# Hybrid decoder trunk: pacing of the last tail, copied scores, and the order of the last four blocks

## The chip, the cores and the metric

The kernel runs on one core of a Trainium2 chip. Time is the device time of one execution in microseconds. The kernel before takes 3587.44 us, the median of three runs (3582.51, 3587.91 and 3587.44). Smaller is better.

## The reference

One pre-norm residual layer over 1024 tokens of width 1024, then a final RMS norm:

```python
h = rms_norm(x, norm_mix[l])
x = x + hybrid_mixer(h, ...)          # stick-breaking attention, sparse attention, HGRN2, gated merge, w_out
h = rms_norm(x, norm_ffn[l])
x = x + peer_ffn(h, peer_w_q[l], peer_sub_keys[l], peer_u[l], peer_v[l])
...
return rms_norm(x, norm_final)
```

The second half is what the change touches. It is a product-key expert layer: each token picks, for each of 8 heads, 16 of 16384 experts, by the 16 best of 128 keys on each of two sides and then the 16 best of the 256 sums.

```python
s = jnp.einsum("nhad,akd->nhak", qh, sub_keys).astype(f32)
top_s, top_i = lax.top_k(s, K)
...
best_s, pos = lax.top_k(cand, K)
eidx = jnp.take_along_axis(cand_idx, pos, axis=-1)
gate = jax.nn.softmax(best_s, axis=-1)
hpre = jnp.einsum("nd,nhkd->nhk", xc, u_tab[eidx]).astype(f32)
act = (gate * jax.nn.gelu(hpre, approximate=False)).astype(x.dtype)
return jnp.einsum("nhk,nhkd->nd", act, v_tab[eidx])
```

## The kernel before

The tokens are four parts of 256 (`PARTS`), eight tiles of 128. The mixer runs first, part by part, as stages whose pieces (projections, norms, scores, routing) are emitted by due times of TensorE and VectorE work; a tail of a part is its merge, output projection, norm, scores and routing. The tail of the last part has nothing of the mixer to lie beside: its 68 steps (8 merges, 22 of projection and norm, 16 of scores, 22 of routing) are put into the list `ending` and handed out during the expert layer.

`score_pieces` makes, for each head, the scores `zs` of two tiles against 128 keys on two sides in PSUM (L973), and VectorE finds the 16 best of each: maximum of eight (L978), their replacement into an SBUF tile `sv` (L980), their indices (L982), and the same again on `sv` (L984, L986). A head has four such sets, so each line runs 128 times over the four parts.

The expert layer is done in two ways. The 512 tokens of parts 1 and 2 (`DENSE`) go over all 16384 experts in 128 blocks of 128: `gemm1` (matmuls at L258, 24 of 128x512 a block, fp16 high and low halves) gives 128 hidden values of 512 tokens, ScalarE takes the Gelu `ge` (L1390), VectorE multiplies it by the gates `gt` (L1424, two instructions), ScalarE and VectorE split it into two fp16 halves `ac` (L213, L214) and the block of `peer_v` likewise into `vs`, and `gemm2` (L1431) adds to the output. `gemm1` runs `LEAD` = 3 blocks ahead. Token tiles 0 to 2 keep their sums in six PSUM banks `accs`; the fourth, for which there is no bank, collects four blocks (`group`), is multiplied in a bank shared with `gemm1`, copied out by ScalarE as `p7` (L1440) and added to `acc7` by VectorE (L1441). At the end the sums are scaled and added to the residual (`yd`, L1460), normed and scaled by `norm_final` (L1462), and stored.

The other 512 tokens (tiles 0, 1, 6, 7 of 128) are done by `gather_tile`, beside the blocks: for each of 128 choices GpSimd gathers 128 rows of `peer_u` by an indirect DMA (L1145, 512 KB), VectorE takes the dot product with the token (L1147); then the same with rows of `peer_v` (L1155), each scaled and added to `gacc` (L1157). Then the sum is normed and multiplied by `norm_final` (L1162) and stored. Rows, the sums `gacc`, the copies of the tokens and `gf` take buffers of the tag `rows`, of which there are five; for tiles 6 and 7 `late_rows` adds seven more places that the mixer has left (names with `rr_` are halves of one of them), in a ring of eleven in which four turns fall to `rows`.

The program is written in this order and a scheduler with a model of the engines arranges the instructions of each engine within what buffers and dependencies allow; VectorE's steps on rows are held back by `paced` to spread them over the blocks. In the loop over blocks, `TP` = 3 steps of `ending` are emitted behind each block. `account` adds a model cost of each VectorE instruction emitted to `load_["DVE"]`. `W2` tiles (the tag `at`, eight buffers) hold `ge`, `sv`, `p7` and the routing's tables.

## Time and profile before

| | |
|---|---|
| median of three runs | 3587.44 us |
| profiled execution | 3598.97 us, span 3597.2 us |
| TensorE busy | 3273.4 us, 91% |
| VectorE busy | 3002.8 us, 83% |
| ScalarE busy | 1588.9 us, 44% |
| GpSimd busy | 1342.3 us, 37% |
| `ac127` to the end | 45.5 us |

The profile lists one execution. Busy time is time in which an engine worked on an instruction; a TensorE that is busy need not run at its peak. The blocks of the expert layer fill the span from about 2150 us on. A wait is put down to the instruction that ended last among those waited for.

### The profile page before, as it was taken

What the parts mean: (1) busy time and instruction counts of PE and PEld (TensorE: products, weight loads), DVE (VectorE), ACT (ScalarE), POOL (GpSimd) and SP (SyncE); (2) the same over time, 40 slices, a digit from 0 to 9 for tenths busy, and PEclk for the clock granted to TensorE, in tenths of its full rate; (3) what the DMA queues carried; (4) which work ended last, traced back from release to release, by engine and by line L of the source; (5) the groups of instructions that cost most, each with busy time, mean ns of one, the idle gap of its engine ahead of it and who ended that gap; (6) DMA issues with size and microseconds to landing.
All of it is one profiled execution on the core that took longest, in us unless ns stands there. A gap on an engine that the chain in (4) does not pass through costs nothing.

```text
span 3597.2 us, 57076 instructions
## 1 busy us (share of the span) xinstructions
PE 3273.4 (91%) x20660; PEld 2191.4 (61%) x20660; DVE 3002.8 (83%) x6662; ACT 1588.9 (44%) x3157; POOL 1342.3 (37%) x1166
## 2 busy tenths in 40 slices
PE   7999989989997889999878879879999999999997
PEld 6887777778875667787666645434444444444443
DVE  5565678888799878788997777999897998898898
ACT  5776455653443554645356333224233333333333
POOL 0000002343323323223332233346674765666664
PEclk9999999999996889999677789989999999999998
DMA  8964856989977577887665799789998999999997
GB/s 300 329 237 143 303 185 224 329 300 328 351 259 230 198 248 244 306 320 261 218 201 184 265 348 316 240 270 374 358 369 316 383 378 343 379 358 364 352 343 263
DMA packets 358760, 1053.88 MB, mean 293 GB/s; under 512 B 35174, under 2 KB 107562, under 8 KB 354380
## 3 DMA queue, kind: packets, MB, share of 16 engines
q0 software_dynamic: 147456, 536.94, 41.7%
q1 hardware_dynamic: 211020, 513.29, 40.2%
q8 instruction: 162, 2.65, 0.3%
q14 instruction: 122, 1.00, 0.1%
HBM read 942.09 MB, written 108.00 MB: 292 GB/s over the span
## 4 chain that ended last, share of the span: by engine, by line
PE 44%; DVE 24%; DMA 11%; issue 10%; ACT 7%; POOL 4%; SPq 0%; POOLq 0%; DVEq 0%; ACTq 0%
PE g L258 11%; PE acc L1431 8%; DVE u L1147 4%; PE pj_mg L258 3%; DVE gacc L1157 3%; PE g L1431 3%; DMA d_G<-stage 3%; PE pj_r_hg L258 3%; DMA v<-in_peer_v_dram,gidx 2%; PE pb L258 2%; DMA u<-in_peer_u_dram,gidx 2%; PE pj_wo L258 2%; POOL v L1155 2%; DMA gt<-d_G 1%; POOL u L1145 1%
## 5 line engine op out<-in xcount | busy, mean ns | idle before, releaser
L1155 POOL DMA_INDIRECT v<-in_peer_v_dram,gidx x421 | 541.5, 1286 | 723.1 <-DVE gacc L1157 435.6
L1145 POOL DMA_INDIRECT u<-in_peer_u_dram,gidx x417 | 523.7, 1256 | 683.2 <-DVE u L1147 440.2
L258 PE MATMUL g<-h,us 128*128 128x512 f16 x3072 | 692.0, 382 | 26.3 <-DVE ts L982 10.3
L1157 DVE SCALAR_TENSOR_TENSOR gacc<-v,act,gacc 128x1024 f32<-128x1024 f32 x421 | 538.5, 1279 | 35.1 <-DMA v<-in_peer_v_dram,gidx 31.6
L1431 PE MATMUL acc<-vs,ac 128*128 128x512 f16 x2304 | 540.3, 383 | 23.1 <-DVE vs L214 9.7
L1431 PEld LDWEIGHTS <-ac 128*128 128x128 f16 x3072 | 303.2, 99 | 419.2 <-issue 58.7
L258 PEld LDWEIGHTS <-us 128*128 128x128 f16 x3072 | 302.1, 98 | 395.3 <-issue 24.8
L1147 DVE SCALAR_TENSOR_TENSOR u<-u,gh 128x1024 f32<-128x1024 f32 x417 | 501.6, 1218 | 33.1 <-DMA u<-in_peer_u_dram,gidx 30.0
L1390 ACT ACTIVATE ge<-g 128x512 f32<-128x512 f32 x128 | 76.2, 595 | 570.6 <-PE g L258 528.2
L258 PE MATMUL pj_mg<-hT,w_mg 128*128 128x256 f16 x2304 | 276.3, 276 | 8.8 <-ACT mg L883 7.0
L258 PEld LDWEIGHTS <-w_mg 128*128 128x128 f16 x2304 | 228.7, 100 | 40.1 <-issue 12.6
L1431 PE MATMUL g<-vs,ac 128*128 128x512 f16 x768 | 187.4, 386 | 24.6 <-ACT ge L1390 23.0
L1221 ACT ACTIVATE stage<-gb 128x512 f32<-128x512 f32 x128 | 130.3, 1070 | 125.3 <-DMA d_G<-stage 59.9
L214 DVE SCALAR_TENSOR_TENSOR vs<-vraw,vs 128x1024 f16<-128x1024 f32 x128 | 155.5, 1218 | 35.5 <-ACT vs L213 35.3
L213 ACT ACTIVATE vs<-vraw 128x1024 f16<-128x1024 f32 x128 | 133.0, 1046 | 82.4 <-DMA vraw<-in_peer_v_dram 79.6
L258 PE MATMUL pb<-o,w_b 128*128 128x256 f16 x1152 | 147.8, 286 | 21.4 <-DVE sg L921 12.7
L1145 POOL DMA_INDIRECT rr_u<-in_peer_u_dram,gidx x95 | 132.6, 1396 | 85.6 <-DVE rr_u L1147 62.7
L1155 POOL DMA_INDIRECT rr_v<-in_peer_v_dram,gidx x90 | 128.6, 1428 | 95.5 <-DVE gacc L1157 72.4
L214 DVE SCALAR_TENSOR_TENSOR us<-uraw,us 128x1024 f16<-128x1024 f32 x128 | 155.9, 1218 | 9.8 <-ACT us L213 9.4
L1218 PE MATMUL gb<-hot 128*128 128x128 f16 x512 | 125.3, 294 | 42.1 <-ACT stage L1221 22.3
L213 ACT ACTIVATE ac<-ge 128x512 f16<-128x512 f32 x128 | 79.7, 627 | 176.0 <-DVE ge L1424 122.3
L1424 DVE TENSOR_TENSOR ge<-ge,gt 128x256 f32<-128x256 f32 x256 | 98.6, 422 | 68.0 <-ACT ge L1390 46.2
(1143 smaller groups left out, 6439.4 us busy)
## 6 DMA issues: line engine op xcount, KB each, us to landing
uraw<-in_peer_uT_dram SPq DMA_DIRECT2D x128, 512.0 KB
vraw<-in_peer_v_dram SPq DMA_DIRECT2D x128, 512.0 KB
w_mg<-dw SPq DMA_DIRECT2D x72, 512.0 KB
d_G<-stage SPq DMA_DIRECT2D x32, 1024.0 KB
gt<-d_G SPq DMA_DIRECT2D x32, 1024.0 KB
w_r_hg<-dw SPq DMA_DIRECT2D x36, 512.0 KB
w_b<-dw SPq DMA_DIRECT2D x72, 256.0 KB
wr_mg<-in_wblk_dram SPq DMA_DIRECT2D x24, 512.0 KB
```

The lines of the kernel that those rows point to most:

```text
L213: S.activation(hi, src, AF.Copy, scale=scale)
L214: V.scalar_tensor_tensor(lo, in0=src, scalar=scale, in1=hi, op0=ALU.mult, op1=ALU.subtract)
L258: P.matmul(ps, l[:, k, :], r[:, k, :], start=(i == 0), stop=(i == n - 1))
L1145: G.indirect_dma_start(out=ur, out_offset=None, in_=a["peer_u"], in_offset=bass.IndirectOffsetOnAxis(ap=idx[:, c:c + 1], axis=0))
L1147: V.scalar_tensor_tensor(ur, in0=ur, scalar=1.0, in1=h2, op0=ALU.mult, op1=ALU.mult, accum_out=hpre[:, c:c + 1])
L1155: G.indirect_dma_start(out=vr, out_offset=None, in_=a["peer_v"], in_offset=bass.IndirectOffsetOnAxis(ap=idx[:, c:c + 1], axis=0))
L1157: V.scalar_tensor_tensor(acc, in0=vr, scalar=act[:, c:c + 1], in1=acc, op0=ALU.mult, op1=ALU.add)
L1218: P.matmul(ps[:, n, :], hs[:, 0, :, n], hs[:, 2, :, n], start=True, stop=False)
L1221: S.activation(stage[0][:, :, m0:m0 + 4].rearrange("p i n -> p n i"), ps, AF.Copy, scale=SA / SGT)
L1390: S.activation(ge, ps, AF.Gelu, scale=1.0 / (SW * SH2))
L1424: V.tensor_tensor(gv, gv, gt[:, :, i % 8, :], op=ALU.mult)
L1431: P.matmul(ps, ac[:, x, t * 128:(t + 1) * 128], v[:, y, dh * 512:(dh + 1) * 512], start=start and n == 0, stop=stop and n == 2)
```

## The change

There are four parts. First, ScalarE copies the scores `zs` out of PSUM into a new SBUF tile `zc`, and VectorE's searches read that. Second, steps of `ending` are handed out by VectorE's model cost: at most `TP` behind a block, and only while those of this block have cost less than `TV` = 6.0 (an excess is carried into the next block). Third, the last four blocks (124 to 127) have no second products of their own: behind block 126 the products of tiles 3 and 0 with blocks 124 to 126 are made, behind block 127 those of tiles 3 and 0 with block 127 and then all four blocks for tiles 1 and 2; the final sums follow in the order 3, 0, 1, 2. Fourth, tiles 6 and 7 take `gfd`, the row `norm_final` that the dense tiles load in the last block, in place of a load of their own into a `rows` buffer.

```diff
--- before.py
+++ after.py
@@ -25,7 +25,8 @@
 
 PACE0, PACE, PB = 135, 420, 3.0
 
-TP, LEAD = 3, 3
+
+TP, TV, LEAD = 3, 6.0, 3
 
 EVERY = 2
 
@@ -972,6 +973,9 @@
             for tl in range(pt.nt):
                 P.matmul(zs[:, tl, :], st["pq", h][:, tl * 128:(tl + 1) * 128], keys, start=True, stop=True)
 
+            zc = W2(f"zc{pt.i}_{h}", (128, pt.nt, 256))
+            S.activation(zc, zs, AF.Copy)
+            zs = zc
             sv = W2(f"sv{pt.i}_{h}", (128, pt.nt, 256))
             four = [(zs[:, tl, x * 128:x * 128 + 128], sv[:, tl, x * 128:x * 128 + 128], st["ts"][:, tl, h, x, :], st["ti"][:, tl, h, x, :]) for tl in range(pt.nt) for x in range(2)]
             for z, v, t, i in four:
@@ -1158,7 +1162,7 @@
         with tc.high_priority():
             log_exp()
         y = rms_scale(acc, f"fin{ti}", rows(f"sqf{ti}"), "g")
-        gf = load(rows(f"gf{ti}"), a["norm_final"].to_broadcast([128, D]))
+        gf = gfd if ti // 2 == PARTS[-1].i else load(rows(f"gf{ti}"), a["norm_final"].to_broadcast([128, D]))
         V.scalar_tensor_tensor(acc, in0=acc, scalar=y, in1=gf, op0=ALU.mult, op1=ALU.mult)
         nc.sync.dma_start(out[ti * 128:(ti + 1) * 128, :], acc)
 
@@ -1405,7 +1409,8 @@
 
     gts = {}
     ys = []
-    gone = 0
+    spare = 0.0
+    pend = {}
     for k, i in enumerate(order):
         if k + LEAD < NI:
             ges[order[k + LEAD]] = gemm1(order[k + LEAD])
@@ -1430,7 +1435,22 @@
             for n, (x, y) in enumerate(((0, 0), (0, 1), (1, 0))):
                 P.matmul(ps, ac[:, x, t * 128:(t + 1) * 128], v[:, y, dh * 512:(dh + 1) * 512], start=start and n == 0, stop=stop and n == 2)
 
-        for u in range(6):
+        if k >= NI - 4:
+
+            last = k == NI - 1
+            for t in ((3, 0) if k == NI - 2 else (3, 0, 1, 2) if last else ()):
+                for dh in range(2):
+                    if t == 3 and dh not in pend:
+                        pend[dh] = ps_mm.tile([128, TH], F32, tag="mm", name=f"g2_{i}_{dh}")
+                    ps = pend[dh] if t == 3 else accs[t * 2 + dh]
+                    todo_ = group if t in (1, 2) else group[3:] if last else group
+                    for x, y in todo_:
+                        gemm2(ps, t, dh, x, y, t == 3 and x is group[0][0], last and x is ac)
+                    if t == 3 and last:
+                        part = W2(f"p7_{i}_{dh}")
+                        S.activation(part, ps, AF.Copy)
+                        V.tensor_tensor(acc7[:, dh], acc7[:, dh], part, op=ALU.add)
+        for u in range(6 if k < NI - 4 else 0):
             if u in (2, 4) and len(group) == 4:
                 d0 = u // 2 - 1
                 ps = ps_mm.tile([128, TH], F32, tag="mm", name=f"g2_{i}_{u}")
@@ -1449,11 +1469,15 @@
                 ys.append(load(W4("yd3"), d_x2[DENSE[0].ti0 + 3]))
                 gfd = load(late.tile([128, D], F32, tag="v", name="gfd", bufs=6), a["norm_final"].to_broadcast([128, D]))
 
-        while ending and gone < (k + 1) * TP:
-            ending.pop(0).emit(1 << 20)
-            gone += 1
+        account()
+        spare, left = TV + min(spare, 0.0), load_["DVE"]
+        for _ in range(TP):
+            if ending and spare > load_["DVE"] - left:
+                ending.pop(0).emit(1 << 20)
+                account()
+        spare -= load_["DVE"] - left
     log_exp()
-    for t in range(4):
+    for t in (3, 0, 1, 2):
         y = ys[t]
         for dh in range(2):
             yv = y[:, dh * 512:(dh + 1) * 512]
```

Line numbers in the changed kernel are up to 24 higher: the dot products are at L1151, the sums of v rows at L1161, the last scaling at L1166, the gates at L1429, the splits at L214 (ScalarE) and L215 (VectorE).

The first place is VectorE's list beside blocks 17 and 18, where the routing of tile 6 (`rt6`, L1042 to L1064) and the sum of tile 1 (`gacc_1`) go. Before, the multiplication of block 18's Gelu by its gates stands here:

```order
L1058 CAST selh0_rt6_24739<-fb_rt6_24439 128x128
L1047 CAST fa_rt6_24438<-ua_rt6_24440 128x128
L1157 SCALAR_TENSOR_TENSOR gacc_1_33887<-v1_117_34240,act_1_33499,gacc_1_33887 128x1024
L1060 TENSOR_TENSOR oneh0_rt6_24741<-selh0_rt6_24739,iota16r_138 128x2048
L1048 COPY_PREDICATED fb_rt6_24439<-ua_rt6_24440,fa_rt6_24438 128x128
L1157 SCALAR_TENSOR_TENSOR gacc_1_33887<-v1_118_34243,act_1_33499,gacc_1_33887 128x1024
L1062 TENSOR_TENSOR oneh0_rt6_24741<-oneh0_rt6_24741,tir0_rt6_24737 128x2048
L1058 CAST selh1_rt6_24750<-fb_rt6_24439 128x128
L1016 MAX_INDEX ua_rt7_24827<-fa_rt7_24825,cand0_rt7_24828 128x8 x4
L1424 TENSOR_TENSOR ge18_24853<-ge18_24853,gt16_0_25013 128x256
L1424 TENSOR_TENSOR ge18_24853<-ge18_24853,gt16_16_25015 128x256
```

In the changed kernel these rows stand about the same multiplication:

```order
L1161 SCALAR_TENSOR_TENSOR gacc_1_33951<-v1_104_34265,act_1_33563,gacc_1_33951 128x1024
L1047 TENSOR_SCALAR ua_rt6_24596<-ua_rt6_24596 128x128
L1161 SCALAR_TENSOR_TENSOR gacc_1_33951<-v1_105_34268,act_1_33563,gacc_1_33951 128x1024
L1048 TENSOR_SCALAR fa_rt6_24594<-ua_rt6_24596 128x128
L1161 SCALAR_TENSOR_TENSOR gacc_1_33951<-v1_106_34271,act_1_33563,gacc_1_33951 128x1024
L1429 TENSOR_TENSOR ge18_24883<-ge18_24883,gt16_0_25034 128x256
L1049 COPY_PREDICATED fb_rt6_24595<-ua_rt6_24596,fa_rt6_24594 128x128
L1050 TENSOR_SCALAR ua_rt6_24596<-ua_rt6_24596 128x128
L1429 TENSOR_TENSOR ge18_24883<-ge18_24883,gt16_16_25036 128x256
L215 SCALAR_TENSOR_TENSOR us22_25267<-uraw22_25265,us22_25267 128x1024
L1161 SCALAR_TENSOR_TENSOR gacc_1_33951<-v1_107_34274,act_1_33563,gacc_1_33951 128x1024
L1051 CAST fa_rt6_24594<-ua_rt6_24596 128x128
```

and these about that of block 19:

```order
L1027 MAX_INDEX ua_rt7_24983<-fa_rt7_24981,cand0_rt7_24984 128x8 x4
L1161 SCALAR_TENSOR_TENSOR gacc_1_33951<-v1_115_34298,act_1_33563,gacc_1_33951 128x1024
L1062 CAST selh0_rt6_24803<-fb_rt6_24595 128x128
L1051 CAST fa_rt6_24594<-ua_rt6_24596 128x128
L1429 TENSOR_TENSOR ge19_24997<-ge19_24997,gt16_0_25034 128x256
L1429 TENSOR_TENSOR ge19_24997<-ge19_24997,gt16_16_25036 128x256
L1161 SCALAR_TENSOR_TENSOR gacc_1_33951<-v1_116_34301,act_1_33563,gacc_1_33951 128x1024
L1064 TENSOR_TENSOR oneh0_rt6_24805<-selh0_rt6_24803,iota16r_138 128x2048
L1052 COPY_PREDICATED fb_rt6_24595<-ua_rt6_24596,fa_rt6_24594 128x128
L215 SCALAR_TENSOR_TENSOR ac19_25302<-ge19_24997,ac19_25302 128x512
```

The multiplication of `ge18` stood behind the last table step on `fb_rt6` before the one-hot tables; it now stands in the first half of these steps, and `ge19` stands where `ge18` did.

The second place is VectorE's list where tile 6 is scaled by `norm_final` (the row with `gy_fin6`). Before:

```order
L214 SCALAR_TENSOR_TENSOR vs76_29177<-vraw76_29175,vs76_29177 128x1024
L225 TENSOR_SCALAR gms_fin6_35033<-gss_fin6_35030 128x1
L214 SCALAR_TENSOR_TENSOR vs77_29237<-vraw77_29235,vs77_29237 128x1024
L230 TENSOR_TENSOR gu_fin6_35038<-gy_fin6_35035 128x1
L231 TENSOR_TENSOR gu_fin6_35038<-gu_fin6_35038,gms_fin6_35033 128x1
L232 TENSOR_SCALAR gu_fin6_35038<-gu_fin6_35038 128x1
L233 TENSOR_TENSOR gy_fin6_35035<-gy_fin6_35035,gu_fin6_35038 128x1
L1162 SCALAR_TENSOR_TENSOR gacc_6_34665<-gacc_6_34665,gy_fin6_35035,gf6_35043 128x1024
L1424 TENSOR_TENSOR ge78_29051<-ge78_29051,gt72_0_28904 128x256
```

and in the changed kernel:

```order
L215 SCALAR_TENSOR_TENSOR vs126_32551<-vraw126_32549,vs126_32551 128x1024
L215 SCALAR_TENSOR_TENSOR ac126_32556<-ge126_32403,ac126_32556 128x512
L1161 SCALAR_TENSOR_TENSOR gacc_7_35481<-rr_v7_82_35715,act_7_35117,gacc_7_35481 128x1024
L215 SCALAR_TENSOR_TENSOR vs127_32601<-vraw127_32599,vs127_32601 128x1024
L1461 TENSOR_TENSOR acc7_23115<-acc7_23115,p7_123_4_32486 128x512
L1166 SCALAR_TENSOR_TENSOR gacc_6_34729<-gacc_6_34729,gy_fin6_35099,gfd_32679 128x1024
L1161 SCALAR_TENSOR_TENSOR gacc_7_35481<-rr_v7_82_35715,act_7_35117,gacc_7_35481 128x1024
L1429 TENSOR_TENSOR ge127_32495<-ge127_32495,gt120_0_32256 128x256
L1429 TENSOR_TENSOR ge127_32495<-ge127_32495,gt120_16_32258 128x256
L1161 SCALAR_TENSOR_TENSOR gacc_7_35481<-rr_v7_84_35720,act_7_35117,gacc_7_35481 128x1024
```

The scaling stood between blocks 77 and 78 and took a row `gf6`; it now takes `gfd` and stands between the splits of block 126 and the gates of block 127, so that `gacc_6` keeps its buffer until there.

The third place is VectorE's list from the split `ac127` on, the last that TensorE waits for. The names `v7_113` and `rr_v7_84` are rows of the last tile, counted from 0 to 127; a name with `rr_` stands for two neighbouring rows. Before:

```order
L1157 SCALAR_TENSOR_TENSOR gacc_7_35419<-v7_112_35737,act_7_35055,gacc_7_35419 128x1024
L214 SCALAR_TENSOR_TENSOR vs124_32465<-vraw124_32463,vs124_32465 128x1024
L214 SCALAR_TENSOR_TENSOR ac127_32558<-ge127_32431,ac127_32558 128x512
L1157 SCALAR_TENSOR_TENSOR gacc_7_35419<-v7_113_35740,act_7_35055,gacc_7_35419 128x1024
L1157 SCALAR_TENSOR_TENSOR gacc_7_35419<-v7_114_35743,act_7_35055,gacc_7_35419 128x1024
L214 SCALAR_TENSOR_TENSOR vs125_32493<-vraw125_32491,vs125_32493 128x1024
L1157 SCALAR_TENSOR_TENSOR gacc_7_35419<-rr_v7_115_35746,act_7_35055,gacc_7_35419 128x1024 x2
L1157 SCALAR_TENSOR_TENSOR gacc_7_35419<-rr_v7_117_35751,act_7_35055,gacc_7_35419 128x1024 x2
L1157 SCALAR_TENSOR_TENSOR gacc_7_35419<-v7_119_35756,act_7_35055,gacc_7_35419 128x1024
```

and in the changed kernel:

```order
L1161 SCALAR_TENSOR_TENSOR gacc_7_35481<-rr_v7_84_35720,act_7_35117,gacc_7_35481 128x1024
L215 SCALAR_TENSOR_TENSOR ac127_32606<-ge127_32495,ac127_32606 128x512
L1161 SCALAR_TENSOR_TENSOR gacc_7_35481<-rr_v7_84_35720,act_7_35117,gacc_7_35481 128x1024
L1161 SCALAR_TENSOR_TENSOR gacc_7_35481<-v7_86_35725,act_7_35117,gacc_7_35481 128x1024
L1161 SCALAR_TENSOR_TENSOR gacc_7_35481<-v7_87_35728,act_7_35117,gacc_7_35481 128x1024
L1161 SCALAR_TENSOR_TENSOR gacc_7_35481<-v7_88_35731,act_7_35117,gacc_7_35481 128x1024
L1452 TENSOR_TENSOR acc7_23115<-acc7_23115,p7_127_0_32612 128x512
L1161 SCALAR_TENSOR_TENSOR gacc_7_35481<-v7_89_35734,act_7_35117,gacc_7_35481 128x1024
L1484 SCALAR_TENSOR_TENSOR yd0_32547<-acc0_23109,yd0_32547 128x512
L1452 TENSOR_TENSOR acc7_23115<-acc7_23115,p7_127_1_32618 128x512
```

Row 113 was the first behind `ac127`; now it is row 85. The rest of the list to row 127 stands behind it in both, the last 25 rows of the changed kernel without another instruction between them.

## Rows read from the trace of the kernel before

**Rows 1.** The page's first part: busy time of each engine over the whole span, its share, and the number of instructions.

```profile
PE 3273.4 (91%) x20660; PEld 2191.4 (61%) x20660; DVE 3002.8 (83%) x6662; ACT 1588.9 (44%) x3157; POOL 1342.3 (37%) x1166
```

**Rows 2.** The span cut into stretches. Columns: start and end, length, busy time (and number of instructions) of TensorE, of its weight loads, of VectorE, ScalarE and GpSimd, then the granted clock of TensorE, the busy share of the DMA engines and GB/s. The stretches end at the splits `ac` of blocks 19, 31, 119 and 127 on VectorE.

```profile
2280.40:2416.80 136.40, 103.55 (x479) 49.07 (x478) 131.84 (x405) 36.94 (x48) 54.75 (x41) 0.87 0.77 249
2416.80:2541.30 124.50, 120.24 (x551) 54.10 (x550) 122.48 (x250) 48.42 (x65) 81.92 (x60) 0.99 0.97 358
2541.30:3463.70 922.40, 908.37 (x4186) 410.53 (x4185) 828.80 (x1106) 304.83 (x405) 586.16 (x409) 0.99 0.97 359
3463.70:3551.70 88.00, 82.36 (x372) 36.66 (x371) 78.99 (x83) 23.21 (x32) 51.99 (x41) 0.98 0.93 332
3551.70:3597.20 45.50, 22.10 (x88) 9.16 (x87) 37.69 (x60) 14.37 (x27) 7.35 (x8) 0.75 0.51 203
```

**Rows 3.** TensorE's timeline, its last instructions. Columns: start, duration, engine, line, operation, tiles, sizes, count, and in brackets the idle time before it with what ended it.

```profile
3579.62 1.03 PE L1431 MATMUL acc<-vs,ac 128*128 128x512 f16 x4
```

**Rows 4.** VectorE's timeline from block 127's split to the end; columns as in rows 3.

```profile
3549.41 1.28 DVE L1157 SCALAR_TENSOR_TENSOR gacc<-v,act,gacc 128x1024 f32<-128x1024 f32 x1
3550.60 1.22 DVE L214 SCALAR_TENSOR_TENSOR vs<-vraw,vs 128x1024 f16<-128x1024 f32 x1
3551.74 0.68 DVE L214 SCALAR_TENSOR_TENSOR ac<-ge,ac 128x512 f16<-128x512 f32 x1
...
3561.31 6.57 DVE L1157 SCALAR_TENSOR_TENSOR gacc<-v,act,gacc 128x1024 f32<-128x1024 f32 x5
...
3592.09 1.28 DVE L1462 SCALAR_TENSOR_TENSOR yd<-yd,y_find,gfd 128x1024 f32<-128x1024 f32 x1
```

**Rows 5.** TensorE's timeline from 2245 to 2435 us, the groups ahead of which it idled or which ran slowly, and one that did neither (2410.93); columns as in rows 3.

```profile
2251.79 5.35 PE L1431 MATMUL g<-vs,ac 128*128 128x512 f16 x24 [1.64 <-DVE ts L982]
...
2290.47 2.78 PE L258 MATMUL pj_pq<-h_last,w_pq 128*128 128x256 f16 x24 [0.69 <-ACT ge L1390]
...
2317.79 7.44 PE L258 MATMUL g<-h,us 128*128 128x512 f16 x24 [10.27 <-DVE ts L982]
...
2391.15 5.28 PE L1431 MATMUL g<-vs,ac 128*128 128x512 f16 x12 [21.89 <-ACT ge L1390]
2396.23 3.21 PE L1431 MATMUL acc<-vs,ac 128*128 128x512 f16 x12
...
2410.93 5.34 PE L258 MATMUL g<-h,us 128*128 128x512 f16 x24
...
2428.30 6.79 PE L258 MATMUL g<-h,us 128*128 128x512 f16 x24 [4.26 <-ACT ge L1390]
```

**Rows 6.** ScalarE's waits from 2105 us to the end. Columns: what waits, what for, us in total, times, the longest.

```profile
ACT vs L213 <- DMA vraw<-in_peer_v_dram: 79.6, 26, 12.0
...
ACT ge L1390 <- DVE fb_rt L1048: 26.6, 1, 26.6
```

**Rows 7.** VectorE's groups from 3551.7 us to the end. Columns: line, engine, operation, out<-in, sizes, count, busy time, mean ns of one, idle time before them.

```profile
L1460 DVE SCALAR_TENSOR_TENSOR yd<-acc,yd 128x512 f32<-128x512 f32 x8 | 5.3, 685 | 1.1 <-PE acc L1431 1.1
L1462 DVE SCALAR_TENSOR_TENSOR yd<-yd,y_find,gfd 128x1024 f32<-128x1024 f32 x4 | 5.0, 1280 | 0.0
...
L1441 DVE TENSOR_TENSOR acc<-acc,p 128x512 f32<-128x512 f32 x2 | 1.4, 684 | 0.0
L1162 DVE SCALAR_TENSOR_TENSOR gacc<-gacc,gy_fin,gf 128x1024 f32<-128x1024 f32 x1 | 1.3, 1282 | 0.0
```

**Rows 8.** ScalarE's timeline, the steps on the last gathered tile's sum of squares; columns as in rows 3.

```profile
3575.22 1.06 ACT L223 ACTIVATE sqf<-gacc 128x1024 f32<-128x1024 f32 x1 [9.38 <-DVE gacc L1157]
...
3579.19 0.20 ACT L228 ACTIVATE gy_fin<-gy_fin 128x1 f32<-128x1 f32 x1
```

**Rows 9.** The page's fifth part, GpSimd's issues of gathered v rows; columns as in rows 7.

```profile
L1155 POOL DMA_INDIRECT v<-in_peer_v_dram,gidx x421 | 541.5, 1286 | 723.1 <-DVE gacc L1157 435.6
...
L1155 POOL DMA_INDIRECT rr_v<-in_peer_v_dram,gidx x90 | 128.6, 1428 | 95.5 <-DVE gacc L1157 72.4
```

**Rows 10.** VectorE's groups over the whole span: the dot products with u rows, and the scores' searches; columns as in rows 7.

```profile
L1147 DVE SCALAR_TENSOR_TENSOR u<-u,gh 128x1024 f32<-128x1024 f32 x417 | 501.6, 1218 | 33.1 <-DMA u<-in_peer_u_dram,gidx 30.0 <-DMA gh<-d_h 1.8 <-issue 1.0
...
L982 DVE FIND_INDEX8 ts<-ts,zs 128x8 uint32<-128x128 f32 x128 | 34.8, 287 | 0.0
...
L986 DVE FIND_INDEX8 ts<-ts,sv 128x8 uint32<-128x128 f32 x128 | 34.5, 281 | 0.0
L1147 DVE DVE_READ_ACCUMULATOR u<-u,gh 128x1 f32 x417 | 33.5, 80 | 0.0
...
L984 DVE MAX8 ts<-sv 128x8 f32<-128x128 f32 x128 | 29.1, 274 | 0.0
L978 DVE MAX8 ts<-zs 128x8 f32<-128x128 f32 x128 | 29.0, 278 | 0.0
```

**Rows 11.** ScalarE's groups over the whole span: copies of a 128x512 tile out of PSUM; columns as in rows 7.

```profile
L1440 ACT ACTIVATE p<-g 128x512 f32<-128x512 f32 x64 | 37.7, 589 | 80.9 <-PE g L1431 74.0 <-issue 4.7 <-DVE ac L214 2.2
```

**Rows 12.** TensorE's waits over the whole span, those that searches of the scores ended in the mixing stages; columns as in rows 6.

```profile
PE zs L973 <- DVE ts L982: 2.9, 4, 1.7
...
PE tra_sb L433 <- DVE ts L982: 1.7, 1, 1.7
```

**Rows 13.** VectorE's waits from 2105 us to the end; columns as in rows 6.

```profile
DVE gacc L1157 <- DMA v<-in_peer_v_dram,gidx: 10.6, 10, 2.1
```

## The prediction

> **What bounds the kernel now.** I read the page's first part, then the span cut into stretches, then the timelines and waits of the stretches that the edits touch. TensorE is busy 91% and VectorE 83% of 3597.2 us [rows 1], but these are means over unlike stretches [rows 2]. Between 2280.4 and 2416.8 us VectorE is busy 131.8 of 136.4 us and TensorE only 103.6: VectorE bounds. From 2541.3 to 3463.7 us TensorE is busy 908.4 of 922.4 us, 908.37/4186 = 0.217 us a matmul: TensorE bounds, and VectorE idles for 93.6 us. After block 127's split, `ac127`, at 3551.7 us, TensorE has 88 matmuls left and ends at 3580.65, while VectorE works on to 3593.4 and the last output lands by 3597.2 [rows 2 to 4]: VectorE and the end chain bound. So a microsecond of VectorE work is worth up to one in the first and the last stretch and nothing in the middle one, and what counts most is how many gathered rows stand behind `ac127`.
>
> Where TensorE stands idle early: 21.9 us before block 15's second product, behind a Gelu of ScalarE that itself waited 26.6 us for the routing's `fb_rt` to give its buffer back; 10.3 and 1.6 us behind the index searches of the scores (they read PSUM, and the gemms share these buffers); 4.3 and 0.7 us behind Gelus [rows 5, 6]. Together 38.8 us. Four groups there also ran slowly, by 2.1, 1.5, 2.5 and 0.5 us against 5.34 for 24 matmuls: 6.6 us, at a granted clock of 0.87 in that stretch against 0.99 later [rows 2, 5].
>
> **The change part by part.** All sums are made against the profiled execution, span 3597.2 us (its own time is 3598.97); the median of the three runs, 3587.44, is 11.5 us (0.32%) below that, and I carry the difference over to it.
>
> *The end.* Before, v rows 113 to 127 of the last tile stand behind `ac127`: 15. Now rows 85 to 127 do: 43, 28 more. The cause lies in the `gfd` edit more than in the pacing. At block 77 the two lists are three rows apart; the other 25 fall back in tile 7, and there the changed kernel keeps `gacc_6`, one of the five `rows` buffers, until `gfd` is loaded in the last block, where before tile 6 was scaled beside block 78. Four of each eleven rows of tile 7 come from these five. Price: rows in a run take 6.57/5 = 1.31 us each, a row between other work 1.19 to 1.20 from start to start [rows 4]. Of the 43, 25 now stand in one run at the very end and 18 between other steps: 25 x 1.31 + 18 x 1.20 = 54.4. Beside them VectorE has the split itself 0.6, two additions 1.2, eight final sums 8 x 0.6, four scalings 4 x 1.2 and some 2 us of 128x1 steps, 13.4 by the spacing of such steps, a little below their rows' durations [rows 7]; the vs splits that stood there are now ahead. That makes 67.8 us from `ac127` to the last row. Then the end chain, which before lay beside the other tiles' work: ScalarE from 3575.22 to 3579.39, 4.2 us [rows 8], five small VectorE steps 0.7, the scaling 1.28 [rows 7], and from the last VectorE end to the span's end 3597.2 - 3593.4 = 3.8 [rows 4]: 10.0. Together 77.8 against 45.5: **+32.3**. TensorE's new order costs nothing beside it: behind `ac127` it has 60 matmuls, 13.0 us, and `gemm1` of block 127 stands as far from TensorE's end as before (96 matmuls). Bounds: +27 if all rows go at 1.20 and two of the small steps are covered, +42 if rows come as slowly as GpSimd issues them, 1.29 to 1.43 us [rows 9], and a few are late.
>
> *The VectorE stretch.* Tile 6's u rows are paced later: 10 fewer stand before block 23's split and 9 fewer before block 31's, and 15 small steps fewer before block 23, none fewer by 31. Such a row is 1.22 + 0.08, a small step about 0.28 [rows 10]: 13.0 + 4.2 = 17 us at block 23, 11.7 at block 31. TensorE takes the lead over between the two (120.2 of 124.5 us busy from 2416.8 on [rows 2]), so I take **-14**, bounds -20 and -8. I count nothing of the 21.9 us stall beyond this: `ge18` now goes through amid the first table search, but `ge19` stands behind as many VectorE steps as `ge18` did, and what ends later is VectorE's work.
>
> *Scores copied.* 32 copies of 128x512 at 589 ns [rows 11] are 18.8 us on ScalarE, which is busy 44% [rows 1]; they lie beside VectorE's work, but give each head one more turn between engines. In exchange PSUM comes free without the searches: in the mixing stages 2.9 and 1.7 us of waits [rows 12]; the 10.3 and 1.6 us [rows 5] belong to the VectorE stretch and are in the -14. I take **-4**, bounds -10 and +5. For the reading itself the nearest rows are the same operations on scores in PSUM and on their copy in SBUF: maximum 278 and 274 ns, index search 287 and 281 [rows 10]. About 5 ns for each of 384 instructions: **-1.9**.
>
> A page speaks for far more here: the Trainium skill's "Perfetto Trace Analysis", section "Optimizing Scalar/DVE Operations", puts VectorE's access overhead at about 60 ns an instruction on SBUF and 125 on PSUM. By the page 384 x 65 ns = 25 us would go, as an estimate; this trace does not agree, since the paired rows differ by 4 and 6 ns.
>
> *The TensorE stretch.* The matmuls are the same in number. 14.0 + 5.6 us of idling are left there [rows 2], and ScalarE's waits for vraw loads come to 79.6 us [rows 6]. With 25 rows fewer competing for DMA, at 0.97 of its time [rows 2], some of that could go; with one row buffer fewer, VectorE may wait for rows (10.6 us in all before [rows 13]) and pass it on. I take **0**, bounds -14 and +10. Two loads of `norm_final` fewer: 0, they are issues of SP only.
>
> Sum: 32.3 - 14 - 4 - 1.9 + 0 = **+12.4**, so 3587.4 + 12.4 = 3600 us.
>
> **The rivals.** *It cancels.* TensorE gains 20 us early and 8 of the 19.6 us of late stalls, because 25 rows fewer move ahead of `ac127`, and the scores give their full 6: 32 - 20 - 8 - 6 = -2, about 3585. For it: DMA busy 0.97 at 359 GB/s in that stretch. Against: a wait of VectorE for rows works the other way.
>
> *It gets faster.* All 38.8 us of early idling, the 6.6 us of slow groups and 10 us late go: 32 - 45 - 10 - 2 = -25, about 3562. For it: the scores no longer hold PSUM, and ending steps are rationed by VectorE's time. Against: VectorE is busy 132 of 136 us there, so TensorE's idling can hardly shrink by more than VectorE's work does, 17.
>
> *Slower by much more.* Tile 7 with one buffer fewer: a row is asked for later, VectorE stands in order before the next Gelu's multiplication, and TensorE starves in blocks 78 to 127. It decides once VectorE's slack of that half, about 47 of the 93.6 us, is used up: 1 us more for each of 50 blocks. Price: 15 to 20 us on top, 3615 to 3620. Against: 25 rows fewer are done there, 32 us of VectorE work.
>
> *Reading PSUM is dear after all.* Should each of the 384 instructions lose a quarter of its 278 to 287 ns [rows 10], 70 ns, 27 us of VectorE work go, mostly in the mixing stages, instead of 1.9: 3600 - 25 = 3575. The paired rows leave it little. This is about the size that the Trainium skill's page named above would make of it.
>
> **How the numbers follow.** Forecast, slower by 8 to 22 us (3595 to 3610): 0.45. Cancels: 0.26. Much slower: 0.12. Faster: 0.14. Reading PSUM dear: 0.03. A measurement of this kernel can tell 0.2%, 7.2 us, from no change. Faster takes its two cases, 0.17; same the cancelling one and the forecast's lower edge, 0.27; slower the rest, 0.56. The range, 3575 to 3618, leaves out the best of the faster case and the worst of the much slower one.
>
> **What would show it.** VectorE from `ac127` to the end about 78 us with 43 rows, TensorE done long before; tile 6's scaling within 10 us ahead of `ac127`; no wait for index searches at the gemms and at zs, but still one long wait behind a Gelu near block 16; the time up to block 31 shorter by about 14 us; blocks 32 to 127 unchanged. Wrong if `ac127` to the end takes under 65 us, if the time up to `ac127` shrinks by more than 30 us, or if VectorE waits more than 25 us for v rows ahead of it.

## The result and the profile after

The changed kernel takes 3614.31 us (median of six runs, 3607.19 to 3625.9), the kernel before in the same comparison 3584.98 us (3575.88 to 3592.22). The ratio is 1.0086, 95% interval 1.0061 to 1.011: slower by 29 us between the medians, 22 to 39 us by the interval. The profiled execution of the changed kernel took 3607.61 us, span 3605.8 us. That is 8.6 us more than the profiled execution of before, so this pair of profiles shows less than a third of the difference; both lie near an edge of their kernels' runs, on opposite sides: before's 14.0 us above the median of its six, the changed kernel's 6.7 us below. Among the runs below two executions took over 5000 us; the medians and ratios are without them.

The stretches of the changed kernel, cut at the same splits of blocks 11, 19, 31, 119 and 127 as [rows 2] (columns as there):

```profile
2270.00:2391.60 121.60, 103.98 (x482) 49.30 (x481) 119.66 (x383) 38.73 (x52) 43.58 (x36) 0.92 0.79 259
2391.60:2521.80 130.20, 122.50 (x561) 55.14 (x560) 125.72 (x254) 49.75 (x66) 83.53 (x55) 0.97 0.90 324
2521.80:3437.40 915.60, 914.09 (x4235) 414.23 (x4234) 812.18 (x1103) 309.59 (x411) 555.34 (x396) 1.00 0.96 355
3437.40:3530.30 92.90, 78.26 (x335) 33.71 (x334) 73.75 (x79) 19.85 (x29) 47.16 (x38) 0.91 0.83 298
3530.30:3605.80 75.50, 14.59 (x68) 6.41 (x66) 68.79 (x85) 10.03 (x23) 40.76 (x37) 0.62 0.76 285
```

The split of block 127 comes 21.4 us earlier, at 3530.3 instead of 3551.7 us, and the end behind it takes 75.5 us instead of 45.5. In that last stretch TensorE works 14.6 us and VectorE 68.8. VectorE's timeline there, against [rows 4] (columns as in rows 3):

```profile
3530.30 0.69 DVE L215 SCALAR_TENSOR_TENSOR ac<-ge,ac 128x512 f16<-128x512 f32 x1
...
3571.61 9.21 DVE L1161 SCALAR_TENSOR_TENSOR gacc<-v,act,gacc 128x1024 f32<-128x1024 f32 x7
3580.85 5.25 DVE L1161 SCALAR_TENSOR_TENSOR gacc<-rr_v,act,gacc 128x1024 f32<-128x1024 f32 x4
3586.14 9.21 DVE L1161 SCALAR_TENSOR_TENSOR gacc<-v,act,gacc 128x1024 f32<-128x1024 f32 x7
3595.38 2.61 DVE L1161 SCALAR_TENSOR_TENSOR gacc<-rr_v,act,gacc 128x1024 f32<-128x1024 f32 x2
...
3600.63 1.28 DVE L1166 SCALAR_TENSOR_TENSOR gacc<-gacc,gy_fin,gfd 128x1024 f32<-128x1024 f32 x1
```

and TensorE's last row:

```profile
3533.07 11.82 PE L1436 MATMUL acc<-vs,ac 128*128 128x512 f16 x54
```

TensorE is done at 3544.9 us. From then on VectorE has rows of the gather, what is left of the dense tiles' scaling (to 3565 us) and the end chain: 61 us in which TensorE has nothing to do, while GpSimd still issues rows until 3587 us.

Ahead of that, in the early stretch, TensorE's idle times are others than in [rows 5]: its timeline, the groups with such a time in front (columns as in rows 3).

```profile
2285.55 4.45 PE L1436 MATMUL acc<-vs,ac 128*128 128x512 f16 x12 [2.09 <-ACT ac L214]
...
2347.88 6.71 PE L259 MATMUL g<-h,us 128*128 128x512 f16 x24 [9.50 <-ACT ge L1394]
...
2387.81 7.22 PE L259 MATMUL g<-h,us 128*128 128x512 f16 x24 [6.02 <-ACT ge L1394]
...
2415.68 6.94 PE L1436 MATMUL g<-vs,ac 128*128 128x512 f16 x24 [7.70 <-ACT ge L1394]
```

The 21.9 us behind one Gelu and the 10.3 us behind the index searches are gone; 9.5, 6.0 and 7.7 us behind three Gelus stand in their place.

Last, between the splits of blocks 77 and 127 (2998.0 to 3530.3 us), VectorE now waits for gathered rows (columns as in rows 6):

```profile
DVE gacc L1161 <- DMA v<-in_peer_v_dram,gidx: 27.1, 9, 4.9
DVE ge L1429 <- DMA gt<-d_G: 23.1, 5, 11.6
```

In before, the same stretch has no such wait for rows. The prediction had named "more than 25 us for v rows ahead of it" as a sign that it is wrong, and this sign came.

Up to the split of block 119 TensorE passes these waits by: it is busy 438.4 of the 439.4 us behind block 77's split. In the last eight blocks it stands idle for 14.6 of 92.9 us (before: 5.6 of 88.0). Two of its waits there, and VectorE's wait for a row just ahead of the first of them (columns as in rows 6 and rows 3):

```profile
PE g L1436 <- DVE vs L215: 5.7, 1, 5.7
PE g L259 <- ACT ge L1394: 4.2, 1, 4.2
...
3520.17 1.28 DVE L1161 SCALAR_TENSOR_TENSOR gacc<-v,act,gacc 128x1024 f32<-128x1024 f32 x1 [4.50 <-DMA v<-in_peer_v_dram,gidx]
3521.37 1.22 DVE L215 SCALAR_TENSOR_TENSOR vs<-vraw,vs 128x1024 f16<-128x1024 f32 x1
```

### The profile page after: what moved, and what is told of

It reads as the page before. It is cut to its first block, busy times and chain, and to the rows that moved or that the text cites. A ratio compares the mean times of both kernels' runs of the same rounds, so it can differ in the third digit from the quotient of the medians.

```text
span 3605.8 us, 57109 instructions
## 1 busy us (share of the span) xinstructions
PE 3267.5 (91%) x20660; PEld 2191.3 (61%) x20660; DVE 2999.7 (83%) x6662; ACT 1612.8 (45%) x3192; POOL 1332.2 (37%) x1166
## 5 line engine op out<-in xcount | busy, mean ns | idle before, releaser
L1159 POOL DMA_INDIRECT v<-in_peer_v_dram,gidx x421 | 525.6, 1248 | 764.1 <-DVE gacc L1161 485.1
L1161 DVE SCALAR_TENSOR_TENSOR gacc<-v,act,gacc 128x1024 f32<-128x1024 f32 x421 | 538.1, 1278 | 55.0 <-DMA v<-in_peer_v_dram,gidx 51.4
L1436 PE MATMUL acc<-vs,ac 128*128 128x512 f16 x2304 | 532.5, 382 | 4.5 <-ACT ac L214 4.5
L1151 DVE SCALAR_TENSOR_TENSOR u<-u,gh 128x1024 f32<-128x1024 f32 x417 | 501.6, 1216 | 33.7 <-DMA u<-in_peer_u_dram,gidx 31.9
L214 ACT ACTIVATE ac<-ge 128x512 f16<-128x512 f32 x128 | 79.9, 628 | 313.2 <-DVE ge L1429 273.0
L1436 PE MATMUL g<-vs,ac 128*128 128x512 f16 x768 | 179.3, 384 | 18.7 <-ACT ge L1394 9.7
L214 ACT ACTIVATE vs<-vraw 128x1024 f16<-128x1024 f32 x128 | 132.9, 1047 | 126.5 <-DMA vraw<-in_peer_v_dram 126.5
L215 DVE SCALAR_TENSOR_TENSOR vs<-vraw,vs 128x1024 f16<-128x1024 f32 x128 | 155.3, 1218 | 28.6 <-ACT vs L214 28.6
L215 DVE SCALAR_TENSOR_TENSOR us<-uraw,us 128x1024 f16<-128x1024 f32 x128 | 155.5, 1216 | 8.8 <-ACT us L214 8.8
L1159 POOL DMA_INDIRECT rr_v<-in_peer_v_dram,gidx x90 | 121.4, 1349 | 86.7 <-DVE gacc L1161 64.8
L1429 DVE TENSOR_TENSOR ge<-ge,gt 128x256 f32<-128x256 f32 x256 | 98.2, 419 | 65.6 <-ACT ge L1394 33.7
```

Source lines behind the costliest of these rows:

```text
L214: S.activation(hi, src, AF.Copy, scale=scale)
L215: V.scalar_tensor_tensor(lo, in0=src, scalar=scale, in1=hi, op0=ALU.mult, op1=ALU.subtract)
L1151: V.scalar_tensor_tensor(ur, in0=ur, scalar=1.0, in1=h2, op0=ALU.mult, op1=ALU.mult, accum_out=hpre[:, c:c + 1])
L1159: G.indirect_dma_start(out=vr, out_offset=None, in_=a["peer_v"], in_offset=bass.IndirectOffsetOnAxis(ap=idx[:, c:c + 1], axis=0))
L1161: V.scalar_tensor_tensor(acc, in0=vr, scalar=act[:, c:c + 1], in1=acc, op0=ALU.mult, op1=ALU.add)
L1429: V.tensor_tensor(gv, gv, gt[:, :, i % 8, :], op=ALU.mult)
```

## The experiments

The theory to test: the change loses by one line, the `gfd` in place of tile 6's and 7's own row, since `gacc_6` then holds one of five buffers of tile 7's row ring. The rivals: another part of the change is what costs, or the late scaling itself and its chain. Each ratio is to the kernel before in the same comparison.

**One part undone or alone.** The first run is the changed kernel without the `gfd` line:

```diff
-        gf = gfd if ti // 2 == PARTS[-1].i else load(rows(f"gf{ti}"), a["norm_final"].to_broadcast([128, D]))
+        gf = load(rows(f"gf{ti}"), a["norm_final"].to_broadcast([128, D]))
```

> The changed kernel with one part undone: tiles 6 and 7 load their own row of norm_final again, so tile 6 is scaled beside block 78 and gives its buffer back. On VectorE's list 22 rows stand behind ac127 instead of 43 (15 before the change). Theory A (the held buffer costs the time): ac127 to the end falls from 75.5 us by 21 x 1.31 = 27.5 to about 48 us and the time from 3614 to about 3587 (3580 to 3592); the time up to ac127 stays as in the changed kernel. Rival (the other parts cost it: ScalarE's copies, the pacing, or TensorE's late order): the rows come back ahead of ac127 as VectorE work and the time stays at 3605 to 3618.

Measured: 3581.42 us, ratio 1.0003 (0.9983 to 1.0023). The whole loss of 0.86% is gone when this one line is undone. In the profile the end behind `ac127` takes 49.6 us, and VectorE has no wait for v rows between blocks 77 and 127.

The second is the kernel before with that line alone (the diff above, reversed).

> The kernel before with that one part alone: tiles 6 and 7 take gfd. 34 rows stand behind ac127 instead of 15. Theory A: 19 rows x 1.31 us = 25 us more behind ac127, and the end chain of the last tile is no longer covered: 3610 (3603 to 3617). Rival (the held buffer alone is harmless, since 19 rows fewer ahead of ac127 let TensorE come earlier by as much): 3580 to 3592.

Measured: 3617.47 us, ratio 1.0106 (1.0081 to 1.013), or 38 us (29 to 47): by the time at the upper end of the range that the theory gave, by the ratio above it. 34 rows stand behind `ac127`, as counted, but the end takes 64.8 us, 19 more than before where 25 were expected. More is lost ahead of it: blocks 77 to 127 took 533.4 us here and 532.3 in the changed kernel, against 525.4 in before and 522.4 without the line. VectorE waits 28.0 us for v rows there, and in the last eight blocks TensorE stands 9.6 us behind a VectorE split (8.3 us in the fifth run).

The third is the kernel before with the last four blocks' products by token tiles alone (the part of the change at `if k >= NI - 4`, with the order 3, 0, 1, 2 at the end).

> The kernel before with the last four blocks' second products by token tiles alone. The rows behind ac127 stay 15 and TensorE has as many matmuls behind gemm1 of block 127. Theory A: within 5 us of before (3580 to 3590), perhaps 3 us less since the dense tiles' sums are ready one by one while VectorE still has rows. Rival (products put off to the end make TensorE the last): 8 to 15 us more, with VectorE waiting for TensorE at the final sums.

Measured: 3592.67 us, ratio 1.0016 (0.9997 to 1.0035). That is just above the theory's range. The interval reaches from 1 us less to 13 us more; a gain is not shown, and whether it costs some 5 us stays open. The end takes 49.8 us.

The fourth is the kernel before with the copy of the scores alone:

```diff
+            zc = W2(f"zc{pt.i}_{h}", (128, pt.nt, 256))
+            S.activation(zc, zs, AF.Copy)
+            zs = zc
             sv = W2(f"sv{pt.i}_{h}", (128, pt.nt, 256))
```

> The kernel before with the scores copied by ScalarE alone. Rows behind ac127 stay 15. Theory A: the mixing stages get 5 to 8 us shorter (first split of block 0 at 2143 instead of 2148 us) and this stays to the end: 3579 (3573 to 3585). Rival 1 (the copies cost ScalarE's turn): 3588 or more. Rival 2 (reading PSUM is dear): 3560 to 3570.

Measured: 3578.32 us, ratio 0.9977 (0.9963 to 0.999), 8 us less (4 to 13). The sign and size are the theory's, but not the place: in this profile the expert layer starts (first split of u, block 0) at 2112.9 us, against 2110.3 in before. What TensorE waited for from there to block 31 (columns as in rows 6):

```profile
PE g L1434 <- ACT ge L1393: 23.1, 1, 23.1
PE g L258 <- ACT ge L1393: 7.4, 2, 4.9
```

The wait of 10.3 us for the searches is gone, as it should be; the wait behind the Gelu is still 23.1 us, and from the start of the layer to block 31 it takes 427.2 us, where the run before this one, without the copies, has 427.1. VectorE is the bound there [rows 2], so a wait that TensorE is spared can come back elsewhere.

Over all profiles with 420 rows paced, six with the copies and six without, the layer starts at 2106.0 to 2122.8 us with them (mean 2112.7) and at 2094.6 to 2110.3 without (2101.9): the mixing is no shorter, rather 11 us longer, though VectorE's list there is the same within each six. The copies take ScalarE's turn, the first rival of this run. TensorE's waits for VectorE in the mixing fall from 101 to 110 us to 83 to 92, but its waits for ScalarE rise from 104 to 116 us to 128 to 141. The one that grows most, in before and in this run (columns as in rows 6):

```profile
PE ov_sb L442 <- ACT aT_sb L435: 12.7, 14, 2.1
```

```profile
PE ov_sb L442 <- ACT aT_sb L435: 22.7, 16, 4.7
```

Where the 8 us are gained is not shown. Blocks 31 to 77 take 473.4 to 480.6 us (mean 476.9) with the copies against 480.9 to 486.7 (484.1), but four of the six with copies have the pacing too; the two without it took 480.6 and 478.0. Blocks 77 to 127 take 510.2 us in this run, against 525.4 in before and 519.1 in the run before this one; yet with tile 7's shorter ring, shown below, it is 507.5 us with copies and 508.4 without. One wait that goes is TensorE's for the copy `p7` behind block 32, 2.0 to 6.7 us in five of the six profiles without copies, this line of before among them, and none there in the six with them; with the copies alone a wait of 4.2 us for `p7` stands behind block 12 instead.

```profile
PE g L258 <- ACT p L1440: 6.7, 1, 6.7
```

The pacing alone came later, as the eleventh run:

```diff
-        while ending and gone < (k + 1) * TP:
-            ending.pop(0).emit(1 << 20)
-            gone += 1
+        account()
+        spare, left = TV + min(spare, 0.0), load_["DVE"]
+        for _ in range(TP):
+            if ending and spare > load_["DVE"] - left:
+                ending.pop(0).emit(1 << 20)
+                account()
+        spare -= load_["DVE"] - left
```

> The kernel before with the ending steps handed out by VectorE's time alone. 20 rows stand behind ac127 (15 before). If the early stretch gives 11 us as in the profiles of the changed kernel and of the run with its own row, and 5 rows more at the end cost 5 x 1.31 = 6.5: 3577 to 3584. Rival (the early gain was a matter of the copies): 3588 to 3596.

Measured: 3591.33 us, ratio 1.0025 (1.0012 to 1.0038), 9 us more: in the rival's range. TensorE's waits from the start of the layer to block 31:

```profile
PE g L258 <- ACT ge L1390: 12.8, 2, 9.1
PE g L258 <- DVE ts L982: 10.3, 1, 10.3
PE g L1431 <- ACT ge L1390: 9.9, 1, 9.9
```

The long wait is divided, but the searches still hold PSUM for 10.3 us, and the stretch takes 435.6 us. With copies and pacing together it takes 415.9 (the changed kernel), 418.4, 417.8 and 420.5 us in four kernels; with the copies alone 427.2 and 429.2. So the early gain, 7 to 13 us on the copies alone, came only with both parts together.

**What in the line costs.** The fifth run keeps everything of before, own rows and the scaling of tile 6 beside block 78, and only holds one buffer:

```diff
         h2 = load(rows(f"gh2_{ti}"), d_h2[ti])
...
+        gf = load(rows(f"gf{ti}"), a["norm_final"].to_broadcast([128, D])) if ti == 7 else None
...
-        gf = load(rows(f"gf{ti}"), a["norm_final"].to_broadcast([128, D]))
+        gf = gf or load(rows(f"gf{ti}"), a["norm_final"].to_broadcast([128, D]))
```

> The kernel before, with tile 7's own row of norm_final loaded at the start of the tile instead of at its end: one of the five rows buffers is held through tile 7, while tile 6 is scaled beside block 78 as before and no one waits for gfd. 36 rows stand behind ac127 (15 before). If the held buffer is what costs: as in the run with gfd alone, about 21 x 1.31 = 27 us behind ac127 and some 25 us of VectorE waits for v rows in blocks 77 to 127, time 3612 to 3628. Rival (the late scaling itself, its wait for gfd or the uncovered end chain): 3580 to 3592.

Measured: 3632.04 us, ratio 1.0126 (1.0103 to 1.0148), 45 us (37 to 53). That is above the range given. No late scaling, no `gfd` for these tiles, and the loss is there, and larger. VectorE waits for v rows between blocks 77 and 127, and behind `ac127` once more; the first row is of the one stretch, the second of the other:

```profile
DVE gacc L1158 <- DMA v<-in_peer_v_dram,gidx: 32.9, 9, 7.7
...
DVE gacc L1158 <- DMA v<-in_peer_v_dram,gidx: 13.2, 4, 6.3
```

The sixth takes the line and gives tile 7 a ring that asks for no more buffers than are free:

```diff
-        j = taken[0] % (RB + 6)
+        m = RB - 2 if name[1] == "7" else RB - 1
+        j = taken[0] % (m + 7)
         taken[0] += 1
 
-        j -= RB - 1
+        j -= m
```

> The kernel before with gfd for tiles 6 and 7, and for tile 7 a ring of ten row places in which three turns fall to the rows buffers instead of eleven with four, so that the ring asks for no more buffers than are free. 22 rows stand behind ac127 instead of 34. If the cost comes from turns that ask for the held buffer: VectorE's waits for v rows ahead of ac127 fall from 28 to under 10 us and the time to 3592 to 3604. Rival (one buffer fewer in flight costs it, whatever the ring): 3610 to 3622.

Measured: 3578.87 us, ratio 0.9986 (0.9967 to 1.0005), better than the theory gave. `gacc_6` is still held and tile 6 is still scaled at the end; yet no wait for v rows is left. The stretch from block 77 to 127 of this kernel, and then that of the run with the held buffer (columns as in rows 2):

```profile
3009.30:3517.80 508.50, 507.78 (x2354) 230.11 (x2353) 463.04 (x627) 164.81 (x221) 326.79 (x231) 1.00 0.98 361
```

```profile
3014.00:3547.30 533.30, 520.13 (x2391) 234.65 (x2390) 450.86 (x615) 166.67 (x222) 317.51 (x222) 0.99 0.93 337
```

With as many buffers held, the DMA engines move 361 instead of 337 GB/s and TensorE hardly stops. So it is not the number of row buffers, but turns of the ring that ask for one that is not free. The traces show what such a turn does to tile 7's u rows: in before VectorE takes them in rounds of eleven, four halves of `rr_` places and seven other rows, up to the end of the tile; in the changed kernel, the second and the fifth run a round has six other rows instead of seven, and the tile ends with 13 such rows in a run, so in each round one row comes late.

The shorter ring without the line was not run, and it may help by itself: from block 77 to 119 its four kernels (sixth, ninth, tenth and twelfth run) took 428.4 to 430.5 us, all kernels with the ring of eleven but the fourth run 437 to 450. In the last eight blocks, though, only a held buffer stands out: 91 to 93 us in its three kernels, 77.7 to 88.0 (mean 81.5) in the eleven others.

The same repair on the whole change is the ninth run (that diff on the changed kernel).

> The whole change, with the ring of ten places for tile 7. 30 rows stand behind ac127 instead of 43. If turns that ask for the held buffer are what the change lost by: ac127 to the end 75.5 - 13 x 1.31 = 58 us, the 27 us of VectorE waits for v rows in blocks 77 to 127 gone, time 3580 to 3592 instead of 3614. Rival (the parts hurt each other in some other way): 3600 or more.

Measured: 3582.62 us, ratio 0.9993 (0.9975 to 1.0012). The end takes 59.6 us, 58 expected, and blocks 77 to 127 take 510.0 us. With the first run this confirms the cause on the kernel itself.

**Are rows behind `ac127` the price of the end?** The seventh run takes the copies and has VectorE do 440 instead of 420 rows beside the mixing stages:

```diff
-PACE0, PACE, PB = 135, 420, 3.0
+PACE0, PACE, PB = 135, 440, 3.0
```

> The kernel before with scores copied by ScalarE, and 440 instead of 420 rows paced beside the mixing stages (constant PACE). One row stands behind ac127 instead of 15. If rows behind ac127 are what the end costs: TensorE now sets the end, ac127 to the end about 42 to 45 us instead of 47.7, and the mixing gets up to 16 x 1.2 = 19 us longer only where VectorE bounds it: 3572 to 3582. Rival (each row costs its 1.2 us wherever it stands): 3590 to 3600.

Measured: 3597.14 us, ratio 1.0029 (1.0013 to 1.0046): the rival in the total. In the end itself the theory holds: one row behind `ac127`, and 31.9 us to the end instead of 47.7, less than the 42 to 45 expected. But the mixing is longer, 2152.7 us to the start of the expert layer in this profile, and so are blocks 77 to 127, 527.8 us against 510.2 in the fourth run. The eighth run, with the last blocks' products by token tiles as well:

> The run with 440 rows paced and scores copied, and the last four blocks' second products by token tiles too. One row stands behind ac127. With VectorE free at the end, dense tiles that are ready one by one save part of the end chain: ac127 to the end about 38 to 41 us, 2 to 5 us less than without, 3568 to 3578. Rival (the order of the last products is worth nothing, or TensorE's products come later by it): 0 to 6 us more than without.

Measured: 3596.9 us, ratio 1.0031 (1.0013 to 1.0049), as much as without. The end takes 33.5 us, the mixing 2134.7, blocks 77 to 127 528.6. The stretches of the mixing, of the seventh run and of before (columns as in rows 2):

```profile
0.00:2152.70 2152.70, 1900.36 (x14168) 1558.65 (x14168) 1692.24 (x4543) 1125.07 (x2530) 518.12 (x578) 0.90 0.74 260
```

```profile
0.00:2110.30 2110.30, 1881.52 (x14168) 1548.47 (x14168) 1672.18 (x4523) 1103.01 (x2499) 500.72 (x559) 0.91 0.75 260
```

VectorE has 20 instructions and 20.1 us more to do there, and the mixing got 40 us longer than the mean of the six with copies, in the other profile 22. So the 14 rows taken from behind `ac127` saved 16 us there and cost more ahead of it.

**Do the gains add up?** The tenth run takes the copies and the line with the shorter ring, on the kernel before (the diffs of the fourth, second and sixth run together).

> The kernel before with the scores copied and gfd for tiles 6 and 7 with the ring of ten places. 23 rows stand behind ac127. If the two gains measured alone add up, 8 us and 5 us less: 3568 to 3577, faster than both kernels. Rival (the copies' gain was drawn from runs that differ by as much, or 8 rows more behind ac127 count in full): 3580 to 3590.

Measured: 3578.76 us, ratio 0.9983 (0.9964 to 1.0001), between the two; they don't add up in full. The twelfth is the ninth without the part on the last four blocks.

> The whole change with the ring of ten places and without the part on the last four blocks. 30 rows stand behind ac127. If that part costs some 5 us, as it may by itself: 3 to 8 us less than the run with it, 3575 to 3587. Rival (it helps when VectorE has rows at the end): as much or up to 5 us more.

Measured: 3576.69 us, ratio 0.9983 (0.997 to 0.9997), 6 us less than the ninth, within what the two intervals allow for no difference. It is faster than both kernels, as is the run with the copies alone (0.9977), the smallest of these edits; the intervals of the two overlap.

Over the profiles, the end behind `ac127` goes by the rows that stand there: 31.9 and 33.5 us with 1 row, 45.5 to 49.8 with 15, 49.0 with 20, 49.6 and 50.3 with 22, 51.5 with 23, 59.6 and 59.7 with 30, 64.8 with 34, 80.0 with 36 (13.2 of it the wait shown above) and 75.5 with 43.

## Why the prediction was right or wrong

The direction, slower, and the range, 3575 to 3618, were right; the predicted time of 3600 us was 14 us too low, and the loss of 12.4 us less than half of the measured 29.

The end: predicted +32.3 us with 77.8 against 45.5; measured 75.5, +30.0. From `ac127` to the last row it took 67.7 us (3530.30 to 3597.99), as worked out; the end chain took 7.8 instead of 10.0. The chain of before had two table loads of ScalarE in it, between the rows of [rows 8]; the changed kernel's ScalarE loads a table early in the end, beside the rows, and none behind the last row (two lines of before, then the one of the changed kernel; columns as in rows 3):

```profile
3576.38 1.28 ACT L227 ACT_TABLE_LOAD   x1
3577.90 1.28 ACT L228 ACT_TABLE_LOAD   x1
```

```profile
3533.88 1.28 ACT L98 ACT_TABLE_LOAD   x1
```

The mechanism, tile 7's ring with a held buffer, was shown by the first, second, fifth, sixth and ninth run. That TensorE's new order hides beside it held: it was done 61 us ahead of the end.

The VectorE stretch: predicted -14, and from the start of the expert layer to block 31 it fell from 430.9 to 415.9 us, -15.0; by the means of the four kernels with copies and pacing (418.2) and the five with neither (428.5) it is -10, within the bounds. That the long Gelu wait would merely move was wrong in form: it was divided into three, of which the longest is 9.5 us. That did not change the size. The prediction did not say that it takes the copies and the pacing together, though; each alone gains nothing there (427.2 and 435.6 us, beside 426.6 to 430.9 in five kernels with neither).

The scores: predicted -4 and -1.9. Alone the copies gave 8 us (4 to 13), so the size is near, but by another way than the one foreseen. The waits at zs behind the searches are gone as foreseen, and in the profile pair the layer starts 4.3 us earlier; over twelve profiles it starts 11 us later with copies, beyond the bound of +5, with the waits for ScalarE shown above; what is gained must lie in the blocks behind. The price of a read by its place, on the changed kernel (columns as in rows 7), against [rows 10]:

```profile
L986 DVE FIND_INDEX8 ts<-ts,zc 128x8 uint32<-128x128 f32 x128 | 36.3, 284 | 0.0
...
L988 DVE MAX8 ts<-sv 128x8 f32<-128x128 f32 x128 | 30.7, 277 | 0.0
L982 DVE MAX8 ts<-zc 128x8 f32<-128x128 f32 x128 | 29.3, 276 | 0.0
```

The maximum went from 278 ns on PSUM to 276 on SBUF, the index search from 287 to 284, while the maximum over `sv`, which was in SBUF in both, went from 274 to 277: no difference beyond that scatter. From the start of one such maximum to the start of the next right behind it, it is 198 ns on PSUM and 193 on SBUF, and 207 and 202 for the index search: the 5 ns of the prediction. Reading PSUM is not dear for these instructions. The Trainium skill's "Perfetto Trace Analysis", section "Optimizing Scalar/DVE Operations", puts VectorE's access overhead at about 60 ns an instruction on SBUF and 125 on PSUM. These rows, 5 ns apart, do not agree with it.

The TensorE stretch: "I take 0, bounds -14 and +10". In the pair of profiles the term came out, 1010.4 against 1008.5 us from block 31 to 127, but by luck: opposite effects cancel in it. Blocks 31 to 77 became 8.9 us shorter, blocks 77 to 119 2.1 and the last eight 4.9 us longer. The rival with one buffer fewer held in part, in other places than it said: the three kernels with a held buffer lose nothing clear up to block 119 (439.4, 442.3 and 441.3 us, within the 428.4 to 449.7 of the others) and some 10 us in the last eight blocks. Its price of 1 us for each of 50 blocks did not come, and VectorE's slack was not used up as a whole: it was idle for 86.7 of the 532.3 us. By the stages, then, the line costs the longer end and these 10 us; that waits for rows are what stops TensorE there is read from a few places of the traces, not tried by itself.

So where do the missing 17 us lie? Not in the pair of profiles: there the terms came to -4.3 (predicted -5.9), -15.0 (-14), -1.9 (0) and +30.0 (+32.3), together +8.8 against the predicted 12.4. What failed is the step from one profiled execution to the median, "I carry the difference over": before's profile was slower than its median, the changed kernel's faster, together 20.7 us. Executions of one kernel differ by 16 us and more here. Counted with means over the profiles, the stages add up to the measured loss, as an estimate: mixing +11, from there to block 31 -10, blocks 31 to 127 0 (1008.5 us against 1010.4 and 1005.8 in the two kernels with before's list of VectorE), the end +28 (75.5 against 45.5 and 49.8), together 29. Of the prediction's terms the one that does not fit is then the -4 of the copies: it named the extra turn between engines and bounded it at +5, and the mixing got 11 us longer.

What stays open: what the last blocks' order costs, if anything; where the gain of the copies lies; what pacing and copies do together; how much the shorter ring gives without a held buffer, and with it why the sixth run came out no slower than before although seven more rows stand behind `ac127`.

## What to carry to other kernels

A tile that waits for a constant loaded late holds its buffer all that time; look up whose ring that buffer belongs to, before taking the load out. A ring written by hand over several pools must take no more turns from each than are really free: one turn too many cost 1.06% and 1.26% here, a ring with one place fewer nothing (0.9986). Where an in-order engine outlasts the others at the end, count its instructions behind the last split that the others need; that count gave the end within 3 us in the changed kernel, the first and the ninth run, was 5 to 13 us too high in the second, seventh and eighth, and 8 us too low in the fifth, where waits for rows stood in the end. A sum made from one profile is a sum about that execution: take several before carrying it to a median.

## What the runs showed of the hardware that was not expected

Stages with the same instructions differ between profiles by as much as the edits do: the mixing by 15.7 and 16.8 us among six kernels whose VectorE has the same list there, blocks 77 to 127 by 6.3 us between two such kernels (before and the third run) and by 0.3 us between two others (the ninth and the twelfth). Twenty more rows in the mixing, 20.1 us of VectorE work, made it longer by 40 and 22 us in two profiles than the mean of the six with copies, more than their own time. With the copies, 24 instructions of ScalarE more in the mixing, TensorE waited there some 25 us longer for ScalarE and some 19 us less for VectorE (means of six profiles each).
